# A cross-entropy kernel: one sum per transfer, a 4736-column piece in the ring, and no engine at 64 instructions

## The chip, the cores and the metric

The kernel runs on one core of a Trainium2 chip. The metric is the device time of one execution in microseconds; lower is better. Every execution was also listed with its *span*, from the first instruction of the program to the last, and the time is always longer than the span. That remainder I call *time minus span*.

## The reference

```python
def reference(logits, labels, smoothing):          # logits 256 x 32000, float32
    log_probs = logits - np.max(logits, axis=-1, keepdims=True)
    log_probs = log_probs - np.log(np.sum(np.exp(log_probs), axis=-1, keepdims=True))
    smooth_targets = np.full((batch, num_classes), smoothing / num_classes)
    ...   # the label's own target gets 1 - smoothing on top
    return (-np.sum(smooth_targets * log_probs, axis=-1)).astype(np.float32)
```

Each row needs the sum of its logits, the sum of their exponentials and the logit of its label. Every logit (32.8 MB) has to come in once.

## The kernel before

Two rows lie on each of 128 partitions. The first row comes in four loads of 8000 columns, the second in ten loads that get narrower. For each piece ScalarE makes exponentials and their sum, and VectorE adds the two halves of the piece and accumulates, so that half a piece's columns are one pass.

```python
WIDTHS = (
    (8000, 8000, 8000, 8000),
    (8000, 6272, 4736, 3648, 2688, 2048, 1536, 1216, 1024, 832),
)
RING_MIN = 6000     # loads of at least this width share a ring of three buffers
PIECE = 4032        # widest piece that is worked on at once
WARM_LEFT, WARM_COLS = 4, 256
...
    def sum_logits(xp, w, out):            # VectorE: (left half + right half), accumulated
        h = w // 2
        jd = junk.tile([P, PIECE // 2], FP32, name="jd", tag="jd")
        return nc.vector.scalar_tensor_tensor(out=jd[:, :h], in0=xp[:, :h], scalar=1.0,
            in1=xp[:, h:w], op0=ALU.mult, op1=ALU.add, accum_out=out)

    def sum_exps(xp, w, out):              # ScalarE: exp, accumulated
        ja = turn.tile([P, PIECE], BF16, name="ja", tag="ja")
        nc.scalar.activation(out=ja[:, :w], in_=xp, func=AF.Exp, accum_out=out)
...
    for t, w in enumerate(WIDTHS[r]):      # second row
        xt = load(w, col, ...)             # ring if w >= RING_MIN, else a buffer of its own
        for i in range(k):                 # k = ceil(w / PIECE)
            xp = xt[:, i * (w // k) : (i + 1) * (w // k)]
            part = sum_logits(xp, w // k, ...)
            sum_exps(xp, w // k, to)
        ...
        elif left == 1:                    # beside the 1024 columns
            # done[0]: totals so far; pairs[0]: VectorE's sum of the 1024, ScalarE's of the 1216 columns
            nc.vector.tensor_tensor(out=done[1][:], in0=done[0][:], in1=pairs[0][:], op=ALU.add)
        ...
        if left == WARM_LEFT:              # matmuls whose only use is to warm TensorE's clock
            for i in range(w // WARM_COLS):
                nc.tensor.matmul(warm[:], lhsT=ident[:], rhs=xt[:, ...], start=True, stop=True)
    # finish: logarithm (ScalarE), two transposes (TensorE), copy and last addition (VectorE), store
```

The softmax here doesn't subtract the row's maximum and nothing guards it: scores larger than these inputs give would overflow.

## Time and profile before

| | before |
|---|---|
| time, median of the first 3 runs | 85.12 us (85.11 to 85.42) |
| span of the profiled run | 83.2 us |
| time minus span (11 runs of the first set of experiments) | 1.80 us (1.77 to 1.84) |
| busy: ScalarE / VectorE / TensorE | 59.9 / 38.7 / 8.0 us |
| data moved | 32.8 MB, 394 GB/s over the span |
| instruction records in the span: VectorE / ScalarE | 74 / 65 |

The views are the page (tenths of busy time in 40 slices), the chain of waits (each line: start, duration, what the end of the run waited on), and the timeline (start, duration, engine, line, operation, output and input, and in brackets the idle time before it and what ended it). Each pass with a sum is followed by a short record that reads the sum out of the engine's accumulator. Their lines of before stand in the prediction. I also use records of the trace that these views do not print: the increments of a semaphore (a counter that others wait on) with which a transfer reports its landing (it has landed at its 16th), the start and size of single packets, the ones of the queue that brings instructions above all, and the two *closing drains*, DRAIN records near the end of each engine's list.

### The profile page before, as it was taken

Reading aid. Unit: us, or ns where it says so; the run is one execution under the profiler, and the core shown is the slowest. Engines: PE = TensorE matmul, PEld = TensorE weight load, DVE = VectorE, ACT = ScalarE, POOL = GpSimd, SP = SyncE. Lnnn points to the kernel's source line nnn. Section 1 sums busy time; section 2 is a strip of 40 time slices with the busy share of each in tenths; the row PEclk is TensorE's granted clock in tenths of the full one; section 3 lists DMA queues with packets and bytes.
Section 4 is the critical chain, followed back from the end, with each engine's and each line's share of the span. In section 5 each row is a group of like instructions: output and inputs, shape, how many; then the busy total and the mean of one; then the engine's idle time right before and its main releaser. Section 6 shows DMA issues by size and latency. Waiting matters only on the chain.

```text
span 83.2 us, 250 instructions
## 1 busy us (share of the span) xinstructions
PE 8.0 (10%) x20; PEld 5.4 (6%) x20; DVE 38.7 (47%) x52; ACT 59.9 (72%) x45; POOL 4.6 (6%) x15
## 2 busy tenths in 40 slices
PE   0000000000000000000001010000000000079960
PEld 0000000000000000000000000000000000067720
DVE  0000059600595009910497119923946754755760
ACT  5000059980699809993499909998999999999950
POOL 3202630010000000000000000000000000000010
PEclk9999999999999999999999999999999999999998
DMA  5999998996999699988999799999999999999500
GB/s 123 431 432 423 438 477 385 492 492 292 446 492 492 292 446 492 492 369 369 492 492 400 338 439 398 518 434 401 428 393 400 442 419 416 416 405 413 230 4 0
DMA packets 2259, 32.78 MB, mean 394 GB/s; under 512 B 337, under 2 KB 338, under 8 KB 850
## 3 DMA queue, kind: packets, MB, share of 16 engines
q1 hardware_dynamic: 2018, 30.72, 87.3%
q10 hardware_dynamic: 144, 2.05, 5.8%
q0 software_dynamic: 96, 0.00, 0.1%
q14 instruction: 1, 0.01, 0.0%
HBM read 32.77 MB, written 0.00 MB: 394 GB/s over the span
## 4 chain that ended last, share of the span: by engine, by line
DMA 59%; ACT 34%; DVE 2%; issue 1%; SPq 0%; PE 0%; ACTq 0%; DVEq 0%
DMA xt<-in_logits_dram 59%; ACT ja L189 34%; DVE jd L177 1%; SPq L171 0%; DVE lin_row L201 0%; PE lin_t L199 0%; DVE res L204 0%; DVE lin L288 0%; DVE done L281 0%; ACTq L189 0%; DVEq L204 0%
## 5 line engine op out<-in xcount | busy, mean ns | idle before, releaser
L189 ACT ACTIVATE ja<-xt 128x4000 bf16<-128x4000 f32 (+1 forms) x12 | 40.9, 3409 | 19.2 <-DMA xt<-in_logits_dram 19.2
L177 DVE SCALAR_TENSOR_TENSOR jd<-xt 128x2000 f32<-128x2000 f32 (+1 forms) x12 | 26.0, 2167 | 31.3 <-DMA xt<-in_logits_dram 31.1
L189 ACT ACTIVATE ja<-xl 128x2368 bf16<-128x2368 f32 (+7 forms) x9 | 16.6, 1839 | 0.0
L177 DVE SCALAR_TENSOR_TENSOR jd<-xl 128x1184 f32<-128x1184 f32 (+7 forms) x9 | 10.7, 1184 | 7.0 <-DMA xl<-in_logits_dram 6.8
L295 PE MATMUL warm<-xl,ident 128*128 128x256 f32 x16 | 6.7, 607 | 24.7 <-DMA xl<-in_logits_dram 24.7
L295 PEld LDWEIGHTS warm<-xl,ident 128*128 128x128 f32 x16 | 5.1, 324 | 26.2 <-DMA xl<-in_logits_dram 24.9
L199 PE MATMUL lin_t<-ident,both 128*1 128x128 f32 x1 | 0.4, 370 | 45.5 <-DVE both L226 45.5
L284 POOL TENSOR_TENSOR se_rest<-done,pair 128x1 f32<-128x1 f32 x1 | 0.4, 402 | 60.1 <-DVE done L281 60.1
L199 PEld LDWEIGHTS lin_t<-ident,both 128*1 128x1 f32 x1 | 0.1, 79 | 45.5 <-DVE both L226 45.5
L189 ACT ACTIVATION_READ_ACCUMULATOR ja<-xt 128x1 f32 x12 | 2.2, 187 | 0.0
L125 POOL DMA_INDIRECT gat<-in_logits_dram,flat_idx x2 | 2.0, 994 | 0.7 <-POOL ident masks.py:199 0.4
L92 ACT ACT_TABLE_LOAD x1 | 1.3, 1283 | 0.9 <-PEq L322 0.9
L189 ACT ACTIVATION_READ_ACCUMULATOR ja<-xl 128x1 f32 x9 | 1.6, 182 | 0.0
L177 DVE DVE_READ_ACCUMULATOR jd<-xt 128x1 f32 x12 | 1.0, 82 | 0.0
L201 DVE COPY lin_row<-lin_t 1x128 f32<-1x128 f32 x2 | 0.6, 278 | 0.8 <-PE lin_t L199 0.8
L204 DVE SCALAR_TENSOR_TENSOR res<-lin_row,lse_t 1x128 f32<-1x128 f32 x2 | 0.6, 276 | 0.8 <-PE lse_t L203 0.7
L229 DVE TENSOR_REDUCE both<-esum 128x1 f32<-128x8 f32 x1 | 0.2, 161 | 1.6 <-ACT ja L189 1.6
L148 POOL TENSOR_SCALAR xsum<-gat 128x1 f32<-128x1 f32 x2 | 0.4, 220 | 7.9 <-DMA gat<-in_logits_dram,flat_idx 7.9
L203 PE MATMUL lse_t<-ident,lse 128*1 128x128 f32 x2 | 0.6, 320 | 2.4 <-ACT lse L195 2.4
L105 POOL DMA_DIRECT2D lab<-in_labels_dram x1 | 0.8, 766 | 1.0 <-POOLq L322 1.0
L177 DVE DVE_READ_ACCUMULATOR jd<-xl 128x1 f32 x9 | 0.7, 83 | 0.0
L117 POOL TENSOR_TENSOR flat_idx<-rowoff,lab 128x2 int32<-128x2 int32 x1 | 0.2, 193 | 5.2 <-DMA lab<-in_labels_dram 5.2
(17 smaller groups left out, 2.9 us busy)
## 6 DMA issues: line engine op xcount, KB each, us to landing
xt<-in_logits_dram SPq DMA_DIRECT2D x4, 4000.0 KB, 21.6
xt<-in_logits_dram SPq DMA_DIRECT2D x1, 3136.0 KB, 19.2
xl<-in_logits_dram SPq DMA_DIRECT2D x1, 2368.0 KB
xt<-in_logits_dram SPq DMA_DIRECT2D x1, 2000.0 KB, 11.3
xt<-in_logits_dram ACTq DMA_DIRECT2D x1, 2000.0 KB, 13.0
xl<-in_logits_dram SPq DMA_DIRECT2D x1, 1824.0 KB, 28.3
xl<-in_logits_dram SPq DMA_DIRECT2D x1, 1344.0 KB, 31.1
xl<-in_logits_dram SPq DMA_DIRECT2D x1, 1024.0 KB, 33.1
```

The source lines that it names most:

```text
L92: nc.scalar.add_instruction(mybir.InstLoadActFuncSet(name=nc.get_next_instruction_name(), act_func_set_id=tbl, ins=[], outs=[],))
L105: nc.gpsimd.dma_start(out=lab[:], in_=labels.bitcast(I32).rearrange("(p f) -> p f", p=P))
L125: nc.gpsimd.indirect_dma_start(out=gat[:, r : r + 1], out_offset=None, in_=logits[:], in_offset=bass.IndirectOffsetOnAxis(ap=flat_idx[:, r ...
L148: nc.gpsimd.tensor_scalar(out=xsum[:, 0:1], in0=gat[:, r : r + 1], scalar1=label_weight, scalar2=None, op0=ALU.mult,)
L177: return nc.vector.scalar_tensor_tensor(out=jd[:, :h], in0=xp[:, :h], scalar=1.0, in1=xp[:, h:w], op0=ALU.mult, op1=ALU.add, accum_out=out,)
L189: nc.scalar.activation(out=ja[:, :w], in_=xp, func=AF.Exp, accum_out=out)
L199: nc.tensor.transpose(out=lin_t[:], in_=lin, identity=ident[:])
L201: nc.vector.tensor_copy(out=lin_row[:], in_=lin_t[:])
L203: nc.tensor.transpose(out=lse_t[:], in_=lse[:], identity=ident[:])
L204: nc.vector.scalar_tensor_tensor(out=res[:, :, r : r + 1], in0=lin_row[:], scalar=-c_small, in1=lse_t[:], op0=ALU.mult, op1=ALU.add,)
L284: nc.gpsimd.tensor_tensor(out=se_rest[:], in0=done[1][:, 1:2], in1=pairs[1][:, 1:2], op=ALU.add)
L295: nc.tensor.matmul(warm[:], lhsT=ident[:], rhs=xt[:, i * WARM_COLS : (i + 1) * WARM_COLS], start=True, stop=True,)
```

## The change

The intent: fewer, wider instructions. VectorE sums a whole transfer at once, which needs a larger scratch buffer; the room comes from moving the 4736 columns into the ring. ScalarE takes the 4736 columns in one piece and not two. The warm-up matmuls start one load earlier. As a consequence no engine comes to 64 instruction records within the span.

```diff
-RING_MIN = 6000
-PIECE = 4032
-WARM_LEFT, WARM_COLS = 4, 256
+RING_MIN = 4736
+PIECE = 4736
+WARM_LEFT, WARM_COLS = 5, 256
...
-    def sum_logits(xp, w: int, out: bass.AP):
+    def sum_logits(xt, w: int, out: bass.AP):
         h = w // 2
-        jd = junk.tile([P, PIECE // 2], FP32, name="jd", tag="jd")
+        jd = junk.tile([P, max(WIDTHS[0]) // 2], FP32, name="jd", tag="jd")
...                                  # first row; the second row likewise
+            sum_logits(xt, w, xsums[r][:, t + 1 : t + 2])
             for i in range(k):
                 xp = xt[:, i * (w // k) : (i + 1) * (w // k)]
-                sum_logits(xp, w // k, xsums[r][:, at + 1 : at + 2])
                 sum_exps(xp, w // k, esums[r][:, at : at + 1])
```

More of the change, by code (lines that the diff above doesn't have):

```diff
@@ L136 @@
     pieces = [[-(-w // PIECE) for w in ws] for ws in WIDTHS]
-    assert all(w % (2 * k) == 0 for ws, ks in zip(WIDTHS, pieces) for w, k in zip(ws, ks))
+    assert all(w % 2 == 0 and w % k == 0 for ws, ks in zip(WIDTHS, pieces) for w, k in zip(ws, ks))
     label_weight = c_big / c_small
@@ L144 @@
     for r in range(R):
-        n = sum(pieces[r])
+        n = len(WIDTHS[r])
         xsum = small.tile([P, n + 1], FP32, name=f"xsum{r}", tag=f"xsum{r}")
-        esum = small.tile([P, n], FP32, name=f"esum{r}", tag=f"esum{r}")
+        esum = small.tile([P, sum(pieces[r])], FP32, name=f"esum{r}", tag=f"esum{r}")
         nc.gpsimd.tensor_scalar(
@@ L172, in load @@
         return xt
-    def sum_logits(xp, w: int, out: bass.AP):
+    def sum_logits(xt, w: int, out: bass.AP):
         h = w // 2
-        jd = junk.tile([P, PIECE // 2], FP32, name="jd", tag="jd")
+        jd = junk.tile([P, max(WIDTHS[0]) // 2], FP32, name="jd", tag="jd")
         return nc.vector.scalar_tensor_tensor(
             out=jd[:, :h],
-            in0=xp[:, :h],
+            in0=xt[:, :h],
             scalar=1.0,
-            in1=xp[:, h:w],
+            in1=xt[:, h:w],
             op0=ALU.mult,
@@ L254 @@
         col += w
+        part = sum_logits(
+            xt, w, xsum[:, t + 1 : t + 2] if left > 1 else pairs[1 - left][:, 0:1]
+        )
         k = pieces[r][t]
@@ L258 @@
             xp = xt[:, i * (w // k) : (i + 1) * (w // k)]
-            part = sum_logits(
-                xp,
-                w // k,
-                xsum[:, at + 1 : at + 2] if left > 1 else pairs[1 - left][:, 0:1],
-            )
             if left == 0:
@@ L274 @@
                 nc.vector.tensor_reduce(
-                    out=done[0][:, 0:1], in_=xsum[:, : at + 1], axis=AX.X, op=ALU.add
+                    out=done[0][:, 0:1], in_=xsum[:, : t + 2], axis=AX.X, op=ALU.add
                 )
```

## The prediction

> **What bounds the kernel now.** I read four views, in this order: the page's table of busy tenths, the chain of waits that ended last, the timeline of the last 16 us, and the instruction records of each engine, counted one by one. The page first:
>
> ```profile
> ACT  5000059980699809993499909998999999999950
> DMA  5999998996999699988999799999999999999500
> q1 hardware_dynamic: 2018, 30.72, 87.3%
> q14 instruction: 1, 0.01, 0.0%
> ```
>
> The row DMA is near nine tenths from the second slice to the 37th, the row ACT (ScalarE) has zeros and fours until the 25th slice and only then stays at 9. So transfers set the pace for two thirds of the run. The question is whether ScalarE takes over after that, because that is where the change shortens it. The chain of waits seems to say so:
>
> ```profile
> 38.30 19.17 DMA xt<-in_logits_dram
> 57.56 5.60 ACT ja L189 x3
> 63.20 4.33 ACT ja L189 x3
> 67.58 3.20 ACT ja L189
> ```
>
> I do not take that at its word, since the timeline shows VectorE, which does the same pieces in less time, waiting for the transfer each time and starting in the same moment as ScalarE:
>
> ```profile
> 63.21 1.39 DVE L177 SCALAR_TENSOR_TENSOR jd<-xl 128x1184 f32<-128x1184 f32 x1 [2.01 <-DMA xl<-in_logits_dram]
> ...
> 67.45 0.18 ACT L189 ACTIVATION_READ_ACCUMULATOR ja<-xl 128x1 f32 x1
> 67.58 3.24 ACT L189 ACTIVATE ja<-xl 128x3648 bf16<-128x3648 f32 x1
> 67.59 2.06 DVE L177 SCALAR_TENSOR_TENSOR jd<-xl 128x1824 f32<-128x1824 f32 x1 [1.54 <-DMA xl<-in_logits_dram]
> ...
> 70.83 1.56 DVE L177 SCALAR_TENSOR_TENSOR jd<-xl 128x1344 f32<-128x1344 f32 x1 [1.18 <-DMA xl<-in_logits_dram]
> ...
> 73.31 1.23 DVE L177 SCALAR_TENSOR_TENSOR jd<-xl 128x1024 f32<-128x1024 f32 x1 [0.92 <-DMA xl<-in_logits_dram]
> ```
>
> The brackets give VectorE's idle time and what ended it. The 3648 columns therefore landed at about 67.5, and ScalarE had no earlier start to miss. The widths of the second row are cut so that each piece lands just as ScalarE becomes free; both engines are level to some hundredths of a microsecond. The landing rate confirms it: from 67.59 to 70.83 the 2688 columns landed (2688 x 512 B = 1.376 MB in 3.24 us, 425 GB/s), and the four 8000-column loads that landed from 13.1 to 50.0 moved 16.38 MB in 36.9 us, 444 GB/s with the part of the second load that had come before; between two full loads (21.6, 31.1, 40.6, 50.0 us) it is 4.096 MB in 9.49 us, 432 GB/s. The bound of the whole kernel is one stream of transfers at 410 to 432 GB/s up to 78.9 us, then the last 832 columns (0.88 us of ScalarE) and a short fixed finish.
>
> **What the Trainium skill says.** "DMA: Bandwidth & Descriptors", section "Where 436 GB/s comes from", gives 435.2 GB/s as the ceiling of the ports into SBUF; the 432 GB/s between full loads agrees, so nothing the compute engines do can speed the stream. "VectorE: DVE Perf Modes", section on the TRN2 errata, says that VectorE and ScalarE pay a fixed extra latency per instruction, a single large tile once and many small tiles each time. The trace agrees: (3243 - 2177) / (3648 - 2368) = 0.833 ns a column on ScalarE and about 0.2 us left over. "TensorE: Matmul & The Clock Gate", Part 1, says the clock falls back after an idle window of some 3.4 us. "Runtime: NRT & Kernel Launch", section "Instruction fetch mechanics", says instructions are fetched in 16 KiB blocks by the sequencer's own queue and mostly hidden; the trace has a fetch of 8192 bytes, so the block differs here.
>
> **The change part by part.**
>
> *One two-input sum per transfer.* VectorE does 21 sums, each followed by an accumulator read. After it are 14: five of 4000, one of 3136, one of 2368, and the seven small ones. By the rows, (2242 - 585) / (2000 - 416) = 1.046 ns a column, so a sum of 4000 takes 2.242 + 2000 x 0.001046 = 4.33 us in place of two of 2.24 that are 2.28 apart, 0.2 us less per load. On the path: nothing. VectorE idles 31.1 us for the big loads. What could hurt is a later release of a ring buffer. A sum starting at 40.62 would end with its read at 45.0, and ScalarE holds the same buffer until 47.57 + 0.19 = 47.76. For the first load the sum now needs both half transfers (13.1), ends near 17.6, and ScalarE holds it until 18.48. So the release stays ScalarE's, and the ring's issues at 18.5, 28.75 and 38.3 stay. Zero.
>
> *4736 columns of exponentials in one piece.* Two pieces of 2368 start at 63.20 and 65.38, and the next piece starts at 67.58: 4.38 us. One piece by the slope: 3.243 + 1088 x 0.000833 = 4.15 us, start to start about 4.17. ScalarE is ready 0.2 us earlier, near 67.37. But the 3648 columns land at 67.5 and are startable at 67.58. The gain becomes an idle wait of 0.2 us. On the path: 0 to 0.02 us.
>
> *4736 columns into the ring.* In the order of instructions of both programs SyncE issues the same transfers in the same order. The one with 4736 now waits for the buffer of the fourth 8000-column load, free at 47.76, where it was issued at 38.68. All narrower ones come behind it on the same queue. The issues take 0.33 to 0.43 us and stood 0.47 apart, so six go out from 47.8 to 50.5; the 1024 wait for the landing at 50.0 as before, the 832 for the one at 57.48 as before. Is the queue ever empty? At 47.8 the fifth 8000 has 2.2 us left and the 6272, issued at 38.3, take 7.46 us after it. The stream needs the 4736 only at about 57; the margin is 9 us. Zero.
>
> *Warm-up matmuls one load earlier.* Now ten blocks of 256 columns of the 2688 load, two passes each, 20 passes. Before, 16 took 6.68 us, weight loads 0.427 us apart; 20 take 8.5 us from about 70.8 to 79.4. Before they ended at 79.95, 0.12 us before the final transpose. The idle gap becomes 0.7 us, far below the 3.4 us that the skill names, so the final transposes should keep 0.27 us (the first row's, cold, took 0.37). Zero.
>
> *Instruction counts.* I counted the records: VectorE 74, ScalarE 65, the others 46 or fewer. After the change VectorE loses 14 and ScalarE 2: 60 and 63. The packets of the instruction queue in the trace are six before the span, one at 79.83 (8192 bytes, 0.32 us) and one at 83.54 (0.57 us), after the span's end at 83.2. The 64th instruction of VectorE is the addition at 79.14, of ScalarE the closing drain at 82.88. Both fetches come 0.66 to 0.69 us after such a 64th instruction; I read them as the refills, and both should vanish. In the span the first costs nothing to be seen: VectorE's next instructions follow at once (read 79.73, addition 79.85, copy 80.38 right behind the transpose), and the logits had all landed. The second may cost: the profiled run was timed at 85.01 with a span of 83.2, so 1.8 us lie outside, and this fetch lies in them until 84.1. Estimate from these numbers: 0 to 0.9 us, and I put 0.2 as its mean, because a fetch ahead need not be waited for.
>
> Sum: 0 (sums) - 0.01 (exponentials) + 0 (ring) + 0 (warm-up) - 0.2 (fetch) = -0.2 us, so 85.12 becomes 84.9.
>
> **The rivals.**
> 1. The saved piece reaches the end. For it: the chain names ScalarE for the last third. Against: VectorE's waits on every landing there. It would make 84.9 with the fetch worth nothing, a saving of 0.2 us, so the time alone cannot tell it from my sum; the landings must.
> 2. The ring starves the stream: the 4736 wait for ScalarE, a wait in place of none. For: every narrow transfer is now behind that wait. Against: 9 us of margin. If later issue costs the stream a gap, each microsecond of gap is one of time; a gap of 1 us makes 86.1.
> 3. The fetch is the real cost and something at the end waits for it. For: it ends at 84.1, inside the time outside the span, and the change takes care that no engine comes to 64. Against: no stall in the span at the first. It makes up to 0.9 us: 84.2.
> 4. The clock of TensorE falls in the 0.7 us gap: two transposes cost 0.1 us more each, 85.1 to 85.3. Against: the gap is a fifth of the skill's window.
>
> **Range and chances.** The three runs of before span 85.11 to 85.42, so some 0.2 us of noise. Downward the fetch, upward noise, a cold transpose or a small hiccup of the stream: 84.4 to 85.3. Faster by over 2% needs 83.4, twice what the fetch could give: 2%. Slower by over 2% needs 86.8, a gap of 1.7 us in the stream: 2%. Within 2%: 96%.
>
> **What would show each step right or wrong.** Right: the 3648 columns still start near 67.58 on both engines, and ScalarE, not only VectorE, has an idle time of 0.1 to 0.2 us before them, ended by the transfer. The 4736 is issued near 47.8 and still startable near 63.2. The sums of 4000 take 4.33 us, the exponentials of 4736 take 4.15. The last piece starts near 79.04, the span stays 83.1 to 83.3. No packet on the instruction queue after the start. The final transposes take 0.27 us. Then any gain in time has to lie outside the span. Wrong: if 3648 starts 0.2 us earlier than 67.58 the stream was not the bound; if the DMA row has a hole after the fourth full load the ring starves it; if the span itself shrinks by over 0.2 us then something that I called hidden was on the path.

## The result, and the profile after

| | before | changed |
|---|---|---|
| time, median | 85.12 us (6 runs) | 85.25 us (85.09 to 85.50, 6 runs) |
| ratio to before | 1 | 1.0011 (95% interval 0.9990 to 1.0033) |
| span of the profiled run | 83.2 us | 83.1 us |
| time minus span, mean | 1.80 us | 2.14 us (1.99 to 2.23) |
| instruction records: VectorE / ScalarE | 74 / 65 | 60 / 63 |

A ratio is the mean time of one kernel's fast runs over the mean of the other's fast runs of the same rounds, so it isn't quite the ratio of the medians. By the 2% measure the two are the same, and the changed kernel is the slower by a hair; a later set of rounds gave 1.0022 (1.0003 to 1.0042). The measured 85.25 is 0.35 us above the predicted 84.9, and inside the stated range.

The page of the changed kernel, the rows of ScalarE and DMA and its whole list of queues:

```profile
ACT  5000049990599809994399918998999999999960
DMA  5999999998999899989998998998999999999600
q1 hardware_dynamic: 2018, 30.72, 87.4%
q10 hardware_dynamic: 144, 2.05, 5.8%
q0 software_dynamic: 96, 0.00, 0.1%
```

The DMA row is as full as before: the ring opened no hole. The queue of instructions, which was in the list of before with one packet, is gone from the span. The chain of waits, from 48.31 us on:

```profile
48.31 19.32 DMA xl<-in_logits_dram
...
67.72 3.19 ACT ja L188
...
80.20 0.27 ACT lse L196
...
80.51 0.28 PE lse_t L202
...
80.82 0.28 DVE res L203
```

The chain now names a transfer up to 67.63, where that of before named ScalarE from 57.56 on. Nothing about the stream had changed; it is only that ScalarE now waits there visibly. The end runs through ScalarE's logarithm, where before it ran through VectorE's additions. The timeline shows both places:

```profile
47.93 0.33 SPq L170 DMA_DIRECT2D xt<-in_logits_dram  x1
...
63.35 4.15 ACT L188 ACTIVATE ja<-xt 128x4736 bf16<-128x4736 f32 x1
63.36 2.62 DVE L176 SCALAR_TENSOR_TENSOR jd<-xt 128x2368 f32<-128x2368 f32 x1 [2.22 <-DMA xt<-in_logits_dram]
67.41 0.19 ACT L188 ACTIVATION_READ_ACCUMULATOR ja<-xt 128x1 f32 x1
67.72 3.24 ACT L188 ACTIVATE ja<-xl 128x3648 bf16<-128x3648 f32 x1
67.72 2.06 DVE L176 SCALAR_TENSOR_TENSOR jd<-xl 128x1824 f32<-128x1824 f32 x1 [1.73 <-DMA xl<-in_logits_dram]
...
78.67 0.08 DVE L176 DVE_READ_ACCUMULATOR jd<-xl 128x1 f32 x1
78.86 0.16 DVE L278 TENSOR_TENSOR done<-done,pair 128x2 f32<-128x2 f32 x1
79.08 0.59 DVE L176 SCALAR_TENSOR_TENSOR jd<-xl 128x416 f32<-128x416 f32 x1
```

The 4736 columns take 4.15 us, ScalarE is through at 67.60, and both engines start the 3648 columns at 67.72, when those land (67.63): the piece that was saved is a wait of 0.12 us. The last three lines have to be laid beside the same place of the kernel before:

```profile
78.54 0.08 DVE L177 DVE_READ_ACCUMULATOR jd<-xl 128x1 f32 x1
78.95 0.19 ACT L189 ACTIVATION_READ_ACCUMULATOR ja<-xl 128x1 f32 x1
79.04 0.88 ACT L189 ACTIVATE ja<-xl 128x832 bf16<-128x832 f32 x1
79.14 0.16 DVE L281 TENSOR_TENSOR done<-done,pair 128x2 f32<-128x2 f32 x1 [0.52 <-ACT ja L189]
79.22 0.58 DVE L177 SCALAR_TENSOR_TENSOR jd<-xl 128x416 f32<-128x416 f32 x1
```

The addition follows the accumulator read by 0.19 us in the changed kernel and by 0.60 us in the kernel before. The bracket blames ScalarE, because its read of 78.95 ended at 79.14. But what this addition takes from ScalarE is the sum of the 1216 columns, whose read ended at 78.0; ScalarE's read at 78.95 is of the 1024 columns, which the addition does not use. In the kernel before it is VectorE's 64th instruction record, and 0.69 us later, at 79.83, a packet of 8192 bytes comes in on the instruction queue. ScalarE's 64th, a closing drain, likewise stood at 82.88 where 82.57 was possible, took 137 ns where the same drain takes 14 in the changed kernel, and had its packet at 83.54. In the changed kernel both packets come as well, but at 84.12 and 85.27, after the span's end. This gave the theory that I tested.

**Theory R.** An engine loses some 0.3 to 0.4 us at its 64th instruction, wherever that is, and a refill of instructions follows. The change did not remove the two refills, it moved them behind the span, into closing code that the profile doesn't list but the time includes. (I call the delay and the packet together a refill.) **Theory S**, its rival: the delay at 79.14 is a late semaphore, refills are free, and the difference lies in noise of the stream.

### The profile page after: what moved, and what is told of

The parts are those of the page before. It is cut to its first block, busy times and chain, and to the rows that moved or that the text cites. A ratio compares the mean times of both kernels' runs of the same rounds, so it can differ in the third digit from the quotient of the medians.

```text
span 83.1 us, 243 instructions
## 1 busy us (share of the span) xinstructions
PE 8.4 (10%) x24; PEld 5.9 (7%) x24; DVE 37.7 (45%) x38; ACT 59.8 (72%) x43; POOL 5.4 (6%) x15
## 4 chain that ended last, share of the span: by engine, by line
DMA 64%; ACT 32%; issue 1%; SPq 0%; PE 0%; DVE 0%; ACTq 0%
DMA xt<-in_logits_dram 40%; ACT ja L188 32%; DMA xl<-in_logits_dram 23%; SPq L170 0%; PE lse_t L202 0%; DVE res L203 0%; ACT lse L196 0%; ACTq L188 0%; ACTq L196 0%
## 5 line engine op out<-in xcount | busy, mean ns | idle before, releaser
L188 ACT ACTIVATE ja<-xt 128x4000 bf16<-128x4000 f32 (+2 forms) x13 | 45.0, 3466 | 19.3 <-DMA xt<-in_logits_dram 19.3
L176 DVE SCALAR_TENSOR_TENSOR jd<-xt 128x4000 f32<-128x4000 f32 (+2 forms) x7 | 27.7, 3953 | 34.3 <-DMA xt<-in_logits_dram 34.3
L188 ACT ACTIVATE ja<-xl 128x3648 bf16<-128x3648 f32 (+6 forms) x7 | 12.2, 1745 | 0.1
L176 DVE SCALAR_TENSOR_TENSOR jd<-xl 128x1824 f32<-128x1824 f32 (+6 forms) x7 | 7.9, 1126 | 5.2 <-DMA xl<-in_logits_dram 5.0
L147 POOL TENSOR_SCALAR xsum<-gat 128x1 f32<-128x1 f32 x2 | 1.2, 621 | 7.0 <-DMA gat<-in_logits_dram,flat_idx 7.0
```

The lines of the kernel that those rows point to most:

```text
L147: nc.gpsimd.tensor_scalar(out=xsum[:, 0:1], in0=gat[:, r : r + 1], scalar1=label_weight, scalar2=None, op0=ALU.mult,)
L176: return nc.vector.scalar_tensor_tensor(out=jd[:, :h], in0=xt[:, :h], scalar=1.0, in1=xt[:, h:w], op0=ALU.mult, op1=ALU.add, accum_out=out,)
```

## The experiments

All twelve runs gave correct results. Padding means one-column memsets on VectorE and one-column copies on ScalarE ahead of everything, in the 11 us in which both wait for the first load:

```diff
+    for i in range(NV):
+        nc.vector.memset(pad_v[:, i : i + 1], 0.0)
+    for i in range(NS):
+        nc.scalar.activation(out=pad_s[:, i : i + 1], in_=zero, func=AF.Copy)
```

It is meant to change nothing but the count, and so where the 64th instruction falls. This table sums up the runs but for the two on the ring, e7 and e8, which are told below. The stream is counted from the landing of the first load to that of the last, so that a late start (the first load landed between 13.09 and 13.46) is left out. That column and the next one, from the last landing to the end of the span, are from the profiled run. The time minus span and the time are means over the timed runs; the text on a single run gives the median of its times. Spans are to 0.1 us, which leaves some 0.02 us of rounding in a mean of six.

| kernel | VectorE's refill | ScalarE's refill | stream, us | last landing to end, us | time minus span, us | time, us (before in the same rounds) | ratio (95% interval) |
|---|---|---|---|---|---|---|---|
| before | tail, 79.14 | closing drain | 65.83 | 4.30 | 1.80 | | 1 |
| changed | outside | outside | 65.81 | 4.09 | 2.14 | 85.26 | 1.0011 (0.9990 to 1.0033) |
| changed, again (e9) | outside | outside | 65.81 | 4.11 | 2.11 | 85.33 (85.14) | 1.0022 (1.0003 to 1.0042) |
| before, 40 and 44 padded (e1) | stream | stream | 66.48 | 4.11 | 1.78 | 85.55 (85.12) | 1.0051 (1.0033 to 1.0068) |
| changed, 40 and 44 (e2) | stream | stream | 66.44 | 4.11 | 1.80 | 85.55 (85.12) | 1.0052 (1.0040 to 1.0064) |
| changed, 8 and 0 (e3) | last addition | outside | 65.79 | 4.36 | 1.90 | 85.35 (85.12) | 1.0024 (1.0009 to 1.0040) |
| sums alone (e4) | outside | closing drain | 65.78 | 4.24 | 2.06 | 85.36 (85.12) | 1.0028 (1.0013 to 1.0043) |
| changed, 7 and 4 (e5) | first closing drain | first closing drain | 65.79 | 4.15 | 1.75 | 84.99 (85.15) | 0.9982 (0.9968 to 0.9995) |
| the same again (e10) | first closing drain | first closing drain | 65.76 | 4.17 | 1.80 | 84.97 (85.14) | 0.9978 (0.9961 to 0.9995) |
| changed, 40 and 0 (e6) | stream | outside | 66.18 | 4.11 | 1.90 | 85.70 (85.15) | 1.0065 (1.0046 to 1.0085) |
| changed, 7 and 0 (e11) | first closing drain | outside | 65.75 | 4.16 | 1.90 | 85.13 (85.14) | 0.9998 (0.9984 to 1.0013) |
| sums alone, 7 and 2 (e12) | first closing drain | first closing drain | 65.78 | 4.14 | 1.81 | 84.98 (85.14) | 0.9983 (0.9970 to 0.9996) |

**Both refills into the middle of the kernel before (40 and 44 padding instructions).**

> Kernel before, with 40 one-column memsets on VectorE and 44 one-column copies on ScalarE put into the idle time before the first landing. Theory R (refill): an engine loses about 0.4 us at its 64th instruction, wherever that falls; in the kernel before that was VectorE's addition at 79.14 (ready at 78.7) and ScalarE's closing drain at 82.88 (ready at 82.6). With the padding both 64ths fall between 20 and 50 us, where both engines wait for transfers. Then the addition starts near 78.7, the last sum starts right after its landing, the closing drain takes 14 ns and not 137, no instruction packet lies after 52 us, and the span falls by 0.3 to 0.4 us to about 82.9; the time falls to 84.7 to 84.9 if no engine comes to such a point outside the span. Theory S (it was a late semaphore of ScalarE, and fetches are free): addition still at 79.1, span 83.2, time 85.1.

The mechanism came out, the time did not: it rose to 85.5. The timeline around VectorE's new 64th instruction, the reduction, then the fifth load, then the tail:

```profile
45.15 0.08 DVE L184 DVE_READ_ACCUMULATOR jd<-xt 128x1 f32 x1
45.75 0.16 DVE L233 TENSOR_REDUCE both<-xsum 128x1 f32<-128x9 f32 x1 [0.52 <-DVE jd L184]
...
50.85 2.24 DVE L184 SCALAR_TENSOR_TENSOR jd<-xt 128x2000 f32<-128x2000 f32 x1 [1.84 <-DMA xt<-in_logits_dram]
...
79.29 0.08 DVE L184 DVE_READ_ACCUMULATOR jd<-xl 128x1 f32 x1
79.48 0.16 DVE L288 TENSOR_TENSOR done<-done,pair 128x2 f32<-128x2 f32 x1
...
79.69 0.19 ACT L196 ACTIVATION_READ_ACCUMULATOR ja<-xl 128x1 f32 x1
```

The reduction comes 0.60 us after the read; in the kernel before the same two are 45.07 and 45.26, 0.19 apart. So the delay of 0.41 us goes with the count and not with the instruction. Against theory S the tail's addition now comes 0.19 us after its read and before ScalarE's read of the 1024 columns (79.69) has begun, so it does not wait for that read. Time minus span is still 1.78. ScalarE's 64th, the accumulator read at 44.13, shows no delay; a pass of 3.5 us was running on ScalarE just before it. What I had not thought of is in the line of 50.85: the fifth load landed at 50.82, 10.22 us after the one before it, where every full load had taken 9.49. The two instruction packets lie at 44.64 and 49.33. From there on every landing is late, by 0.65 to 0.72 us, counted from the first landing. A refill under the stream costs the stream.

**The same in the changed kernel.**

> Changed kernel with the same padding. Theory R: its two fetches at 84.12 and 85.27, outside the span, were the same two refills put off into the closing code; with the padding they lie before 52 us, the span stays 83.0 to 83.1 and the time falls by 0.3 to 0.6 us to about 84.8, the best of all kernels. Theory S: time 85.2 as without padding; the fetches after the span belong to other engines and stay.

Time minus span fell from 2.14 to 1.80, as theory R had it, so the fetches at 84.12 and 85.27 were these refills. But the packet at 44.82 lengthened the stream by 0.6 us, and the time rose to 85.5. The second packet, at 62.38, lengthened it by less than 0.1 us more.

**VectorE's 64th instruction on the final chain (8 padding instructions).**

> Changed kernel with 8 memsets on VectorE at the start, so that its 64th instruction is the last addition into the result (56th without them), on the chain that ends last. Theory R: that addition starts 0.3 to 0.4 us later than its operand allows (near 81.2 and not 80.8), the span becomes 83.4 to 83.5. The time rises by 0 to 0.4 us, 85.3 to 85.6: what the span loses the closing code may gain. Theory S: span 83.1, time 85.2.

```profile
80.72 0.27 PE L206 MATMUL lse_t<-ident,lse 128*1 128x128 f32 x1 [0.33 <-ACT lse L200]
...
81.22 0.28 DVE L207 SCALAR_TENSOR_TENSOR res<-lin_row,lse_t 1x128 f32<-1x128 f32 x1 [0.52 <-PE lse_t L206]
```

From the start of the transpose to the addition it is 0.50 us, in the changed kernel 80.51 to 80.82, 0.31: 0.2 us more where 0.3 to 0.4 were expected, since VectorE began its 0.4 us while it was waiting anyway. Last landing to end grew from 4.09 to 4.36. Time minus span fell to 1.90. The span was 83.6, a tenth above the range, and the time 85.36, within it.

**One sum per transfer alone.** Ring, pieces and warm-up stay as before; VectorE has 60 instructions and ScalarE 65.

> The one-sum-per-transfer part alone (ring, pieces of exponentials and warm-up as before): VectorE 60 instructions, ScalarE 65. Theory R: VectorE's tail addition is free of the delay (near 78.7), the last chain goes through ScalarE's logarithm, ScalarE's closing drain is still late by 0.3 us; span 83.1 to 83.3, time 85.1 to 85.3, same as before. Theory of the prediction for the stream: all landings within 0.05 us of those before, once shifted by the first landing. Theory S: same time, addition still at 79.1.

The stream is 65.78 us, the same as before within 0.05. The time of 85.38 is just over the range. The addition follows its read by 0.19 us. Time minus span rose to 2.06: VectorE's refill alone, moved outside, already costs there. From here the parts can be priced, in the span from one profile each. In the span, VectorE's refill in the tail was worth 4.30 - 4.24 = 0.06 us and ScalarE's in the closing drain 4.24 - 4.09 = 0.15 us. Outside, VectorE's costs 2.06 - 1.80 = 0.26 us and ScalarE's 2.14 - 2.06 = 0.08 us. The change thus saved 0.21 us in the span and paid 0.34 us after it.

**Both refills under the result's transfer (7 and 4 padding instructions).** If this is right, both engines should have their 64th instruction where they have nothing to do: at the first closing drain, while the result is on its way out.

> Changed kernel with 7 memsets on VectorE and 4 copies on ScalarE at the start, so that both 64th instructions are the engine's first closing drain, done while the result's transfer is still under way. Theory R (each refill costs its engine some 0.4 us wherever it comes, and moves from the span to the closing code outside when the count is under 64): both are hidden, span 83.0 to 83.2 when the first landing is as in the kernel before, time minus span 1.80 as in the kernel before (measured 1.77 to 1.84 there, 1.99 to 2.23 in the changed kernel); time 84.8 to 84.95, ratio 0.996 to 0.998, faster than both kernels. If the closing code costs the same with or without refill, time 85.2 to 85.3 as the changed kernel.

The span was 83.2, time minus span 1.75, the ratio 0.9982 and the median time 84.96, both a hair above the ranges given, but this is the first kernel faster than the one before, by some 0.2% (interval 0.9968 to 0.9995; by the 2% measure still the same). The queues between 80 and 83 us show both refills there:

```profile
q14 instruction: 2, 0.02, 1.7%
q1 hardware_dynamic: 2, 0.00, 0.1%
```

**VectorE's refill alone under the stream (40 padding instructions).** The second packet had cost nothing in the run with both; either it was hidden behind the first, or VectorE's are cheap.

> Changed kernel with 40 memsets on VectorE alone, so that its refill falls near 62 us under the full stream and ScalarE's stays in the closing code. In the run with both paddings ScalarE's fetch at 44.8 lengthened the landing of the fifth 8000 by 0.6 us and VectorE's fetch at 62.4 the 4736 by 0.08. Theory Q (a fetch takes a place on one DMA engine, that engine stays late, and the second fetch hit another engine that could be late by as much without showing): the landing of the 4736 or the next comes 0.5 to 0.7 us late, all later ones too, span 83.6 to 83.8, time 85.5 to 85.7. Theory Q2 (only a fetch beside 16000-byte packets hurts, or only ScalarE's): the landings shift by 0.1 at most and the time is 85.2.

```profile
57.85 2.82 ACT L192 ACTIVATE ja<-xt 128x3136 bf16<-128x3136 f32 x1 [0.30 <-DMA xt<-in_logits_dram]
58.28 3.43 DVE L180 SCALAR_TENSOR_TENSOR jd<-xt 128x3136 f32<-128x3136 f32 x1 [3.60 <-DMA xt<-in_logits_dram]
...
63.89 4.15 ACT L192 ACTIVATE ja<-xt 128x4736 bf16<-128x4736 f32 x1 [0.33 <-DMA xt<-in_logits_dram]
```

VectorE, whose 64th this sum is, starts 0.43 us after ScalarE on the same columns; the bracket puts that down to the transfer, which ScalarE shows to have landed. The packet came at 61.67. The 4736 landed 6.04 us after the 6272, where the changed kernel has 5.66, and all later landings stay late by the same 0.37 us. So it was hidden behind the first one, and it costs the stream when alone. Why only 0.37, with 0.5 to 0.7 expected? The 16 increments of each landing tell, in order of time:

| landing | 14th | 15th | 16th |
|---|---|---|---|
| changed, 4736 | 63.17 | 63.19 | 63.27 |
| 40 and 44 padded (e2), fifth 8000, after one packet | 50.05 | 50.09 | 50.69 |
| the same run, 4736, after both packets | 63.20 | 63.81 | 63.88 |
| 40 and 0 padded (e6), 6272, before its packet | 57.51 | 57.52 | 57.77 |
| the same run, 4736, after its packet | 63.17 | 63.42 | 63.81 |

In e2 each packet makes one more increment 0.6 to 0.7 us late, and the late ones stay late to the last load; the stream ends with the latest alone. In e6 one increment was 0.25 late in every landing from the first load on, before any packet. Its packet made another one late by 0.64, of which the stream, counted from the first landing, shows 0.37. So the delay is within theory Q's range, and its picture, one late place out of 16 for each fetch, is what the increments show. That such a place is one DMA engine is inferred: neither an increment nor a packet carries its engine's number. The packets beside the fetch were of 18944 bytes here and of 32000 in the fifth 8000 (not 16000, as my expectation says), so no effect of their size is to be seen.

**More loads in the ring (3648 and 2688 too; e7).** The *lead* of a transfer is the time from its issue to the moment when its first packet is due behind a full queue.

> Changed kernel with 3648 and 2688 columns in the ring as well. Their issues wait for the release of the fifth 8000 (57.4) and of the 6272 (63.3); their first packets were due at 62.3 and 66.7, so the lead is 4.9 and 3.4 us where the 4736 had 9. Theory of the prediction (a wait for a buffer costs nothing while the queue holds work for longer than an issue takes to reach it): all landings as in the changed kernel within 0.05 us, time 85.2 to 85.3. Rival (every narrow transfer behind a wait opens a gap): span longer by some 0.5 us.

The 3648 was issued at 57.40 and its first packet ran at 62.32, the 2688 at 63.42 and 66.66. All landings are within 0.03 us of those of the changed kernel, the time is 85.2 (ratio 1.0005, 0.9991 to 1.0019), time minus span 2.11. A wait for a buffer is free at a lead of 3.2 us.

**All loads in the ring (e8).** Here the ring has to bind: each of the last loads can be issued only when the piece three before it is done.

> All transfers in the ring (the warm-up matmuls then read the 1216 columns, so that they hold no buffer that is needed again). The last issues wait for ScalarE's pieces: 1216 near 73.4 with its packets due at 74.3, 1024 near 75.3 (due 75.8), 832 near 76.8 (due 77.1). The first transfer took 1.02 us from issue to its first packet, the result's 0.75. Theory of the prediction: here the lead is under that and the stream gets gaps, of 0.1 to 0.2 us at the 1216 and 0.3 to 0.6 at each of the last two; last landing 0.6 to 1.3 us later, time 85.8 to 86.5. Rival (an issue reaches the engines at once, or the ring is hidden anyway): time 85.2 to 85.3.

It binds, much harder than I expected: 88.33 us, ratio 1.0381 (1.0348 to 1.0414), the only run clear of 2%. ScalarE's pieces of 1536, 1024 and 832 columns:

```profile
76.07 1.48 ACT L187 ACTIVATE ja<-xt 128x1536 bf16<-128x1536 f32 x1 [0.54 <-DMA xt<-in_logits_dram]
...
79.76 1.06 ACT L187 ACTIVATE ja<-xt 128x1024 bf16<-128x1024 f32 x1 [0.71 <-DMA xt<-in_logits_dram]
...
81.80 0.90 ACT L187 ACTIVATE ja<-xt 128x832 bf16<-128x832 f32 x1 [0.88 <-DMA xt<-in_logits_dram]
```

The last load was issued at 77.67, its packets ran from 78.94 to 81.37, it landed at 81.71. I had counted 1.02 us to the first packet and the usual time after that. But the way to the first packet took 1.27 us, the packets 2.43 us where they take 1.48 behind a full queue, and the landing came 0.34 us after the last: 4.0 us from issue to landing for 0.43 MB. Already the 1536, issued at 71.18 when its packets were due at 72.4, landed 0.6 us late. The 2048, issued at 67.72 with its packets due at 69.93, had landed on time. So the lead of 9 us in the changed kernel was ample, and the limit lies between 2.2 and 1.2 us.

**The direct comparison.** The last four runs share a chip and the runs of before.

> The changed kernel unaltered, beside the padded ones on one chip. Theory R in numbers, from the runs so far, where the time splits into last landing, last landing to the end of the span, and span to time: before 4.31 and 1.80, changed 4.09 and 2.14. So time minus span 2.1 to 2.2, last landing to end 4.05 to 4.15, time 85.15 to 85.3, ratio to before 0.9995 to 1.002.

> The changed kernel with both refills at the first closing drain (7 and 4 padding instructions), again, for a direct comparison with the changed kernel on one chip. Theory R: time minus span 1.73 to 1.80, last landing to end 4.10 to 4.20, ratio to before 0.997 to 0.9990, and 0.2 to 0.35 us under the changed kernel. If the first time was luck: ratio 1.000 to 1.002.

> The changed kernel with 7 memsets on VectorE alone: its refill under the result's transfer, ScalarE's in the closing code outside the span. If the two engines' refills outside add up (VectorE's 0.25, ScalarE's 0.1, from the runs where one of them was outside): time minus span 1.88 to 1.92, ratio to before 0.998 to 1.0005. If only the last of them counts: time minus span 2.1.

> One sum per transfer alone (4736 columns in two pieces, in their own buffer, warm-up one load later), with both refills at the first closing drain (7 and 2 padding instructions). Theory of the prediction for the rest (one piece, ring and earlier warm-up are worth nothing): landings and ratio as with the whole change and hidden refills, 0.997 to 0.9995. If the one piece on ScalarE or the earlier warm-up is worth 0.1 to 0.2 us at the end: ratio 0.9995 to 1.001.

The changed kernel unaltered had 85.33 us (mean), with hidden refills 84.97: 0.36 us less in the same rounds, 0.01 over the range that I had given. In between lies the run with VectorE's refill hidden and ScalarE's outside: time minus span 1.90, time 85.13. The costs outside add up (0.1 for ScalarE's, 0.2 to 0.3 for VectorE's). One expectation missed narrowly: the changed kernel's ratio of 1.0022 is above the 1.002 I had given, its mean time above 85.3 by 0.03 us (the median, 85.28, is inside). The last run says what the rest of the change is worth: sums alone with hidden refills give 84.98, the whole change with hidden refills 84.97. Ring, one piece and earlier warm-up are worth nothing measurable.

## Why the prediction was right, and where it was not

- **The bound.** Right. The stream took 65.83 us before and 65.81 after, and the columns that ScalarE got through sooner were waited for, 0.12 us of idle time, within the 0.1 to 0.2 stated. Rival 1 is out.
- **The sums.** Right: a sum of 4000 took 4.32 to 4.33 us (4.33 predicted), and the buffers were still released by ScalarE. Worth nothing.
- **The exponentials of 4736.** Right: 4.15 us as predicted, worth nothing.
- **The ring.** Right: issued at 47.93 (47.8 predicted), startable at 63.35, no gap. The run with all loads in the ring shows that rival 2 is a real danger, at leads near 1 us and not at 9.
- **The warm-up.** Right in effect, off in size. I had taken the 0.427 us between passes as fixed; it was the cold pace, which in the kernel before lasted until the last two passes (79.35 us). In the changed kernel the passes come 0.216 us apart from about 76 us on, so twenty took 7.11 us and not 8.5 and ended at 78.03. The idle time before the transposes is 1.90 us and not 0.7, and they still take 0.27 us. Rival 4 is out.
- **The fetch.** This term failed: "-0.2 us" became +0.1. Two statements in it were wrong. "Both should vanish": they were put off into the closing code, where both together cost 0.34 us. And "in the span the first costs nothing to be seen": it cost VectorE 0.41 us at the addition at 79.14. I overlooked it because I believed the bracket, which named ScalarE; checking which sums the addition reads would have shown the delay in the profile of before. On the path that ends last it was worth only 0.06 us, as ScalarE's logarithm was nearly as late; with ScalarE's closing drain 0.21 us. Rival 3 had the right event and the wrong sign: the closing code does wait for the refill, but the change puts it there.

With the measured term the sum is -0.21 + 0.34 = +0.13 us, 85.12 to 85.25; that this meets the measured time to the hundredth is more than one set of runs can test. The range held because it was wider than every term. The one term that counted had the wrong sign, and that the time still lay under 85.3 was luck.

What stays open: what the refill does in the 0.4 us that it delays the 64th instruction, and why VectorE's costs more outside than ScalarE's. It is not the wait for the packet's data, since the packet runs after the delayed instruction has begun (79.83 against 79.14, and under the full stream 61.67 against 58.28). Each delay on VectorE was after idle time; behind a running pass, as with ScalarE in e1, none was seen. Padding ahead of everything moves an instruction's count and its place in the program together, so the runs do not tell the two apart. I saw it only at a count of 64 records, the first of the program included; in e1 VectorE came to 114 and ScalarE to 109 with one refill each, and I did not look further.

## What to carry to other kernels

Ask of a cost that an edit removes whether it leaves the measured time or only the span: time minus span beside the span told that here within one set of runs. When the releaser that a profile names is not an operand of the waiting instruction, look for something else, such as the instruction's place in its engine's count. A fixed cost that can't be removed can be moved: eleven padding instructions put both refills under the result's store and made the best kernel (0.9978 and 0.9982 of before), while refills under a saturated stream made the stream 0.4 to 0.7 us longer.

## What the Trainium skill lacked or had wrong

- "Runtime: NRT & Kernel Launch", section "Instruction fetch mechanics": it has refills of 16 KiB every 256 instructions, mostly hidden. Here a packet of 8192 bytes comes after an engine's 64th instruction record; that instruction is delayed by about 0.4 us on VectorE (at four different instructions, in five runs), a ScalarE drain by 0.3 us, and a refill after the last instruction of the program still adds 0.1 us (ScalarE) or 0.2 to 0.3 us (VectorE) to the time.
- No page that I read says what a refill does to a full stream of loads. Here each packet of 8192 bytes made one more of the 16 increments of every later landing some 0.5 to 0.7 us late. The stream paid only for the latest: 0.37 to 0.65 us for one packet or two.
- "DMA: Bandwidth & Descriptors", section "Latency and other measured facts", gives about 600 ns to the first byte of a DMA on the HWDGE path (the trace lists these queues as hardware_dynamic). Here it was 1.02 us from the start of the issuing instruction at the program's start, and 1.27 us for the last load of the run with all loads in the ring; from that instruction's end it was 0.62 and 0.94 us, so the first agrees if the page counts from there and the second does not. That load of 0.43 MB took 4.0 us from issue to landing, its packets 2.43 us in place of 1.48 behind a full queue.
